# Fetching the experts' slots by indirect DMA from normed rows in DRAM, in place of one-hot products

## The chip, the cores and the metric

The kernel runs on one core of one Trainium2 chip. The metric is the device time of one execution in microseconds (us). Before the change it was 2628.83 us, the median of 3 runs (2625.51 to 2629.55).

## What is computed

Two transformer blocks on 512 tokens of width 1024, all in float32. The first has a mixer of four kinds of heads and then a mixture of 32 experts; the second has two attention layers. The change touches the mixture of experts alone. Cut to what matters:

```python
def moe(h, router_w, router_b, w_up, b_up, w_down, b_down):      # h: 512 tokens x 1024
    logits = xt @ router_w + router_b                            # 32 experts
    top_vals, top_idx = lax.top_k(logits, 4)                     # 4 experts a token
    gates = softmax(top_vals)
    ...                                                          # sort the token-expert pairs by expert
    def expert_block(e, xb):                                     # xb: the rows of the expert's tokens
        hu = xb @ w_up[e] + b_up[e]                              # 1024 x 2048
        g = minimum(hu[:, :1024], 7.0); lin = clip(hu[:, 1024:], -7.0, 7.0)
        return ((lin + 1.0) * g * sigmoid(1.702 * g)) @ w_down[e] + b_down[e]   # 1024 x 1024
    y = segment_sum(y_rows * row_gate, row_tok)
```

The input `h` is an RMS-normed row, scaled and shifted per channel.

## The kernel before

**Stages.** By the profile's clock the first mixer runs to about 395 us, the experts from there to about 1560 us, the second block to the end. Every expert's weights (12 pieces of 128 x 2048 float32, 1 MB each: 8 for the up product, 4 for the down product) are read from HBM once. SyncE's queue issues these loads (`load_piece`, L201 to L208) in a fixed order. A piece goes to the next of 8 buffers in turn: 2 with the tag `w`, 6 with the tag `w2` (`NW2=6`).

**Kinds of experts.** Experts are ranked by their number of tokens. The first 17 ranks have 128 slots ("wide"), the others 64 ("thin"), and rank 1 has 128 and 64 more ("both"). A wide expert's products (`expert_mm`, L1278 to L1280) use the three-product split: each half piece of weights is cut into a high part by ScalarE (L1262) and a low part by VectorE (L1263), in 3 + 1 buffers each. A thin expert (`thin_mm`, L1292) multiplies the float32 pieces straight from their load buffers, which are thus free when TensorE is done with them.

**Order of the work.** `moe_groups` pairs ranks: one wide unit alone, three pairs wide and thin, one pair "both" and thin, four pairs, one wide alone, seven pairs. For each unit, `moe` issues the first half of the up product, then the down product of the unit before it, then the second half of the up product (`expert_up`, `expert_down`). In the last unit of each group, between that down product and the second half, `make` calls `slot_sets` for the next group. So it is called 16 times in this loop, 14 times in a thin unit and twice in a wide one (the first unit and the wide unit that stands alone), and once ahead of it.

**What `slot_sets` does.** The normed rows of all tokens are kept on chip as a high and a low part, in the tiles `aTh` and `aTl` (2 x 16 KB of each partition; written at L988, L989). For each set a one-hot matrix of tokens against slots is made on VectorE (L1177). 64 matmuls (8 channel chunks, 4 token tiles, 2 parts; L1192) then multiply rows by one-hot columns into four PSUM tiles. ScalarE evicts them with scale and shift (L1200); for a wide set ScalarE and VectorE split the outcome again (L1204, L1205). After the second half of the up product, `slot_index` finds each slot's token and gate with small matmuls (L1219, L1223) and VectorE operations (L1228 to L1233).

**The results.** `expert_down` adds each unit's rows to the output in DRAM with an indirect accumulating DMA from GpSimd's queue (L1376).

**Order on each engine.** The framework that builds the program orders instructions per engine ahead of time by what it reckons to be ready, so neighbouring steps of the listing are interleaved: in the trace the high parts of the next wide unit are made in the midst of the evictions of `slot_sets`.

Of the kernel before, what the change touches and what calls it, by code (L numbers as in the profile page):

```python
# [12 lines left out]
F32 = mybir.dt.float32  # L13
# [7 lines left out]
P = 128  # L21
# [65 lines left out]
class Kern:  # L87
# [13 lines left out]
    def run(self):  # L101
        with self.early():
            self.consts()
            with self.phase("first", NW2=1, NHT=17, NHD=8, NP=8):
                x = self.first_mixer()
            with self.phase("moe", NW2=6, NP=1):
                x, aT, late = self.moe(x)
        with self.phase("second", NW2=0, NHD=19, NP=11):
            self.second_block(x, aT, late)
# [5 lines left out]
        return ctx  # L115

    def phase(self, name, **sizes):
        self.wrr = -1
# [746 lines left out]
    def first_mixer(self):  # L865
# [58 lines left out]
        for k in range(KC):  # L924
# [238 lines left out]
    def width(kind):  # L1163
        return C if kind == "wide" else CN

    def slot_sets(self, sets, mid=iter(())):


        nc = self.nc
        next(mid, None)  # L1170
        n = sum(self.width(kind) for kind, *_ in sets)
        oh = self.t([P, NT, 2 * C], F32R, tag="eoh", bufs=1)[:, :, 0:n]
        xs, at, o = [], [], 0
        for kind, R, *_ in sets:
            w = self.width(kind)
            sh = [P, NT, w]
            nc.vector.tensor_tensor(oh[:, :, o:o + w], self.C["iota1"][:, None, 0:w].to_broadcast(sh),  # L1177
                                    R[:, :, None].to_broadcast(sh), op=OP.is_equal)
            if kind == "wide":
                xs.append(self.t([P, 2, KC, C], F32R, tag="xT", bufs=1))  # L1180
            else:
                xs.append(self.t([P, KC, CN], tag="xN", bufs=3))
            at.append(slice(o, o + w))
            o += w
        next(mid, None)
        for k0, bank in zip(range(0, KC, 2), ("tr", "tr", "o", "o2")):
            pt = self.psum(bank)
            for q in range(2):
                k = k0 + q
# [4 lines left out]
            if k0 == 2:  # L1194
                next(mid, None)
            for (kind, *_), x, a in zip(sets, xs, at):
                f = self.t([P, 2, C], tag="ef", bufs=2) if kind == "wide" else x[:, k0:k0 + 2, :]
                for q in range(2):
                    k = k0 + q
                    nc.scalar.activation(f[:, q], pt[:, q * n + a.start:q * n + a.stop], AF.Identity,  # L1200
                                         scale=self.s2[:, k:k + 1], bias=self.b2[:, k:k + 1])
                if kind == "wide":
                    hi, lo = (x[:, m, k0:k0 + 2, :] for m in range(2))
                    nc.scalar.activation(hi, f, AF.Copy)  # L1204
                    nc.vector.tensor_tensor(lo, f, hi, op=OP.subtract)  # L1205

        def index():
            for (kind, _, tok, dst, gate), a in zip(sets, at):
                self.slot_index(kind, oh[:, :, a], tok, dst, gate)
        return xs, index  # L1210

    def slot_index(self, kind, oh, tok, dst, gate):


        nc = self.nc
# [9 lines left out]
        u = self.t([P, 1], tag="six", bufs=2)  # L1225
        if kind == "wide":
            dump = self.C["dump"]
            nc.vector.tensor_scalar(u, v[:, 1:2], dump, None, op0=OP.mult)  # L1228
            nc.vector.scalar_tensor_tensor(dst, v[:, 0:1], dump, u, op0=OP.add, op1=OP.subtract)
        else:  # L1230
            nc.vector.tensor_scalar(u, v[:, 1:2], self.C["ndd"], self.C["dn2"], op0=OP.mult, op1=OP.add)
            nc.vector.scalar_tensor_tensor(dst, v[:, 0:1], 2.0, u, op0=OP.mult, op1=OP.add)
        nc.vector.tensor_reduce(gate, v[:, 2:4], axis=AXX, op=OP.add)  # L1233
# [172 lines left out]
    def moe(self, xin):  # L1406
# [8 lines left out]
        gates = self.t([P, nset], tag="eix2", bufs=1)  # L1415
        cols = {}

        def make(g, R, tok, mid=iter(())):
# [10 lines left out]
            xs, index = self.slot_sets(sets, mid)  # L1429
            xs = iter(xs)  # L1430
            return {pos: [(kind, next(xs)) for kind, _ in kinds] for pos, kinds in g}, index

        def load(pos, ns):
            if pos not in ex:
# [13 lines left out]
        xs, index = make(groups[0], self.R, self.tok, order)  # L1448
        index()
        for _ in bias:  # L1450
            pass
        starts = {g[-1][0]: n + 1 for n, g in enumerate(groups)}
        prev = None
        for n, (pos, kinds) in enumerate(units):
            aT = []

            def mid():
                aT.extend((kind, self.expert_aT(a) if kind == "wide" else self.thin_aT(a)) for kind, _, a in prev[1])
            sets = [(kind, x, self.t([P, D], tag="ea", bufs=1) if kind == "wide" else self.t([P, 512], tag="eat", bufs=1))
                    for kind, x in xs[pos]]  # L1460
            self.expert_up(0, sets, w, pos, mid if prev else None)
            if not n:
                for _ in order:
                    pass
            if prev:
                self.moe_down(prev[0], aT, load(prev[0], range(8, 12)), cols, dsts, gates)
            g = starts.get(pos)
            if g is not None and g < len(groups):
                more, index = make(groups[g], self.Rp, self.tokp)
                xs.update(more)  # L1470
            else:
                index = None
            wu = load(pos, range(4, 8))
            self.expert_up(1, sets, wu, pos)
            if index:
                index()
            if n == 2:
                self.moe_jobs()
            if n + 1 < len(units):
# [20 lines left out]
    def moe_overflow(self):  # L1500
# [5 lines left out]
        with tc.For_i(0, n, 1):  # L1506
# [5 lines left out]
            xs, index = self.slot_sets([("wide", R, tok, dst, gate)])  # L1512
            index()
# [814 lines left out]
```

## Time and profile before

| | |
|---|---|
| median of 3 runs | 2628.83 us (2625.51 to 2629.55) |
| the profiled execution's own time | 2645.91 us |
| its span, first to last instruction | 2644.0 us |
| TensorE matmul busy (x 15499) | 2512.5 us, 95% of the span |
| VectorE busy | 1768.8 us, 67% |
| ScalarE busy | 1258.2 us, 48% |
| GpSimd busy | 154.2 us, 6% |
| mean granted TensorE clock | 0.929 of full speed |
| moved by DMA | 566.51 MB |

The times below come from one profiled execution, which was 17 us longer than the median of the runs. "Busy" of TensorE counts pipelined matmuls with modelled ends, so the starts of neighbouring matmuls tell their real pace. "Idle before" is the time an engine stood still ahead of an instruction, with what ended it. [...] "DMA share" is the mean busy share of the 16 DMA engines.

### The profile page before, as it was taken

To read this page: it belongs to the slowest core of one execution; us is meant where nothing else is said; L and a number is where in the kernel's file an instruction comes from. 1 tells how busy PE (TensorE), PEld (TensorE's weight loads), DVE (VectorE), ACT (ScalarE), POOL (GpSimd) and SP (SyncE) were. 2 spreads that over 40 slices of the span, in tenths; PEclk is the share of its full clock that TensorE was granted. 3 is DMA by queue.
4 is the path that set the end of the run, shared out by engine and by line. 5 is a ranking of instruction groups with operands and counts; after the bars stand their busy time and mean duration, and the time that the engine had idled before them with its cause. 6 is when DMAs were issued, how large, how long until landed. Compare 5 with 4: busy or idle time off the path is not lost.

```text
span 2644.0 us, 40335 instructions
## 1 busy us (share of the span) xinstructions
PE 2512.5 (95%) x15499; PEld 1988.1 (75%) x15499; DVE 1768.8 (67%) x3369; ACT 1258.2 (48%) x2198; POOL 154.2 (6%) x151
## 2 busy tenths in 40 slices
PE   5998879999999999999999969989999999899998
PEld 5875678777677777777777748777777987777778
DVE  6886666766556665866666645687786656877864
ACT  3443546545345554654445534454554444545542
POOL 1001000100000000100000000010000100100001
PEclk9998788999999999999999979999999999999998
DMA  7531237999789999999999962131112431311124
GB/s 294 200 118 68 69 118 291 347 379 370 285 330 377 377 376 376 350 367 378 374 378 372 380 255 84 50 112 67 64 43 86 163 109 51 111 64 64 43 85 144
DMA packets 85828, 566.51 MB, mean 214 GB/s; under 512 B 9984, under 2 KB 10576, under 8 KB 22144
## 3 DMA queue, kind: packets, MB, share of 16 engines
q1 hardware_dynamic: 76368, 536.55, 52.3%
q0 software_dynamic: 7968, 23.90, 3.8%
q10 hardware_dynamic: 1296, 3.44, 0.3%
q8 instruction: 124, 2.03, 0.3%
q14 instruction: 72, 0.59, 0.1%
HBM read 543.93 MB, written 19.92 MB: 213 GB/s over the span
## 4 chain that ended last, share of the span: by engine, by line
PE 71%; DVE 8%; ACT 2%; issue 2%; POOL 1%; DMA 1%; ACTq 0%; POOLq 0%; DVEq 0%
PE mm L1292 5%; PE s L1292 5%; PE mm L395 5%; PE mm L397 5%; PE mm L396 4%; PE o L1292 4%; PE mm L1278 3%; PE o L1278 3%; PE o L1192 2%; PE tr L1192 2%; PE mm L1279 2%; PE mm L1280 2%; PE s L1278 2%; PE o L1280 2%; PE o L1279 2%; PE s L1279 2%
## 5 line engine op out<-in xcount | busy, mean ns | idle before, releaser
L1262 ACT ACTIVATE wh<-w 128x1024 fp32r<-128x1024 f32 x306 | 317.6, 1061 | 292.8 <-PE mm L1279 185.1
L1263 DVE TENSOR_TENSOR wl<-w,wh 128x1024 fp32r<-128x1024 f32 x306 | 367.3, 1220 | 98.8 <-ACT wh L1262 97.2
L214 DVE TENSOR_TENSOR wl<-w,wh 128x1024 fp32r<-128x1024 f32 x194 | 237.1, 1225 | 157.3 <-ACT wh L213 155.4
L213 ACT ACTIVATE wh<-w 128x1024 fp32r<-128x1024 f32 x194 | 205.1, 1060 | 240.0 <-PE mm L372 111.8
L371 PE MATMUL mm<-wl,aTh 128*128 128x256 f32 x816 | 234.7, 288 | 3.5 <-DVE wl L214 3.5
L370 PE MATMUL mm<-wh,aTh 128*128 128x256 f32 x816 | 234.5, 289 | 1.4 <-ACT wh L213 0.6
L372 PE MATMUL mm<-wh,aTl 128*128 128x256 f32 x816 | 235.0, 289 | 0.8 <-DVE aTl L308 0.8
L395 PE MATMUL mm<-aTh,wh 128*128 128x512 f32 x560 | 225.8, 403 | 1.1 <-DVE hd L431 1.1
L397 PE MATMUL mm<-aTh,wl 128*128 128x512 f32 x560 | 223.5, 399 | 0.0
L396 PE MATMUL mm<-aTl,wh 128*128 128x512 f32 x560 | 222.7, 398 | 0.0
L371 PEld LDWEIGHTS mm<-wl,aTh 128*128 128x128 f32 x816 | 157.8, 193 | 6.4 <-DVE wl L214 4.1
L370 PEld LDWEIGHTS mm<-wh,aTh 128*128 128x128 f32 x816 | 157.3, 193 | 5.1 <-issue 1.7
L372 PEld LDWEIGHTS mm<-wh,aTl 128*128 128x128 f32 x816 | 157.3, 193 | 4.3 <-issue 2.7
L459 ACT ACTIVATE P<-s,smx 128x256 f32<-128x256 f32 (+3 forms) x176 | 92.7, 527 | 79.2 <-DVE smx L456 77.5
L1263 DVE TENSOR_TENSOR spl<-w,sph 128x1024 fp32r<-128x1024 f32 x102 | 124.5, 1221 | 0.4 <-ACT sph L1262 0.4
L395 PEld LDWEIGHTS mm<-aTh,wh 128*128 128x128 f32 x560 | 105.9, 189 | 23.0 <-issue 3.8
L1292 PE MATMUL mm<-w,xN 128*64 128x256 f32 x1024 | 122.5, 393 | 0.0
L1321 DVE TENSOR_SCALAR eg<-s 128x512 f32<-128x512 f32 (+1 forms) x66 | 37.0, 561 | 127.5 <-PE s L1282 92.7
L1292 PE MATMUL s<-w,xN 128*64 128x256 f32 x1024 | 122.0, 392 | 0.0
L397 PEld LDWEIGHTS mm<-aTh,wl 128*128 128x128 f32 x560 | 105.7, 189 | 21.6 <-issue 2.0
L1262 ACT ACTIVATE sph<-w 128x1024 fp32r<-128x1024 f32 x102 | 108.2, 1061 | 26.3 <-PE mm L1279 11.6
L396 PEld LDWEIGHTS mm<-aTl,wh 128*128 128x128 f32 x560 | 105.9, 189 | 18.9 <-issue 1.1
(614 smaller groups left out, 5981.5 us busy)
## 6 DMA issues: line engine op xcount, KB each, us to landing
w<-w_exp SPq DMA_DIRECT2D x384, 1024.0 KB, 9.2
w<-w_in SPq DMA_DIRECT2D x57, 1024.0 KB, 4.9
w<-w_out SPq DMA_DIRECT2D x24, 1024.0 KB, 4.9
w<-ada_w SPq DMA_DIRECT2D x19, 1024.0 KB, 4.9
w<-cmp_w SPq DMA_DIRECT2D x8, 1024.0 KB, 4.8
w<-w_up SPq DMA_DIRECT2D x16, 512.0 KB, 3.3
xm<-hd POOLq DMA_DIRECT2D x5, 512.0 KB, 2.9
aTl<-ada_w SPq DMA_DIRECT2D x2, 1024.0 KB, 8.0
```

The costliest lines, as they stand in the source:

```text
L213: self.nc.scalar.activation(hi, src, AF.Copy)
L214: (self.nc.gpsimd if pool else self.nc.vector).tensor_tensor(lo, src, hi, op=OP.subtract)
L370: nc.tensor.matmul(v[:, q, :], ah[k][:, ts], w_h, start=(k == 0), stop=False)
L371: nc.tensor.matmul(v[:, q, :], ah[k][:, ts], w_l, start=False, stop=False)
L372: nc.tensor.matmul(v[:, q, :], al[k][:, ts], w_h, start=False, stop=(k == kk - 1))
L395: nc.tensor.matmul(ps, w_h, ah[k], start=(k == 0), stop=False)
L396: nc.tensor.matmul(ps, w_h, al[k], start=False, stop=False)
L397: nc.tensor.matmul(ps, w_l, ah[k], start=False, stop=(k == kk - 1))
L1262: nc.scalar.activation(hi, w, AF.Copy)
L1263: (nc.gpsimd if n in self.LO_POOL else nc.vector).tensor_tensor(lo, w, hi, op=OP.subtract)
L1278: nc.tensor.matmul(ps, xh[:, k, :], wh[:, q, :], start=(k == 0), stop=False)
L1292: nc.tensor.matmul(ps[CN * c:CN * (c + 1), 0:256], a, w[:, c * 256:(c + 1) * 256], start=(n == 0), stop=(n == len(jobs) - 1))
```

## The change

- When the rows are normed, GpSimd also writes each normed row tile in float32 to a new DRAM tensor `xg` (512 x 1024).
- The first set is made as before, with one-hot products (`first_set`). After it the two tiles `aTh` and `aTl` hold no rows any more, and are used as four more weight buffers (`self.more`). `NW2` goes from 6 to 4, so there are 10 buffers instead of 8.
- For every other group, `slot_rows` finds the slots' tokens (one-hot matrix, `slot_index`) and fetches their rows by an indirect DMA from `xg`: 128 rows of 4 KB for a wide set; for a thin one 128 half rows of 2 KB, the two halves of 64 tokens. This is done one group ahead, after the second half of the last unit's up product.
- `slot_sets` then only transposes the fetched rows on TensorE (8 transposes for a wide set, 4 for a thin one, into PSUM tiles `tr`, of which there are 2) and evicts them as before. It is called inside the second half of the up product, between its two PSUM banks.

```diff
-            with self.phase("moe", NW2=6, NP=1):
+            with self.phase("moe", NW2=4, NP=1):
...
     def load_piece(self, src):
         self.wrr += 1
-        if self.wrr % (self.NW + self.NW2) < self.NW:
+        n = self.wrr % (self.NW + self.NW2 + len(self.more))
+        if n < self.NW:
             w = self.g([P, 2048], F32, "w", self.NW)
+        elif n < self.NW + self.NW2:
+            w = self.t([P, 2048], tag="w2", bufs=self.NW2)
         else:
-            w = self.t([P, 2048], tag="w2", bufs=self.NW2)
+            w = self.more[n - self.NW - self.NW2]
...
+        self.xg = self.dp.tile([S, D], F32, name=self.nm("xg"), tag="xg")
...
             for q, x in enumerate(xs):
-                hi, lo = (r[:, 2 * tp + q, :] for r in self.rows)
+                t = 2 * tp + q
+                xr = self.row()
+                nc.gpsimd.tensor_scalar(xr, x, rs[:, q:q + 1], None, op0=OP.mult)
+                nc.gpsimd.dma_start(self.xg[t * P:(t + 1) * P, :], xr)
+                hi, lo = (r[:, t, :] for r in self.rows)
...
+    def first_set(self, R, tok, dst, gate, mid):
...
+        for k0, bank in zip(range(0, KC, 4), ("tr", "o")):
+            pt = self.psum(bank)
+            for q in range(4):
                 for t in range(NT):
                     for m, r in enumerate(self.rows):
-                        nc.tensor.matmul(pt[:, q * n:(q + 1) * n], r[:, t, k * P:(k + 1) * P], oh[:, t],
+                        nc.tensor.matmul(pt[:, q * C:(q + 1) * C], r[:, t, (k0 + q) * P:(k0 + q + 1) * P], oh[:, t],
...
+            self.wide_parts(pt, k0, out)
+        self.slot_index("wide", oh, tok, dst, gate)
...
+    def wide_parts(self, pt, k0, out):
+        f = self.t([P, 4, C], tag="eg2", bufs=1)
+        for q in range(4):
+            k = k0 + q
+            nc.scalar.activation(f[:, q], pt[:, q * C:(q + 1) * C], AF.Identity, scale=self.s2[:, k:k + 1],
+                                 bias=self.b2[:, k:k + 1])
+        hi, lo = (out[:, m, k0:k0 + 4, :] for m in range(2))
+        nc.scalar.activation(hi, f, AF.Copy)
+        nc.vector.tensor_tensor(lo, f, hi, op=OP.subtract)
+
+    def slot_rows(self, sets):
+        out = []
+        for kind, R, tok, dst, gate in sets:
+            n = self.t([P, 1], I32, tag="eig", bufs=4)
+            self.slot_index(kind, self.one_hot(kind, R), tok, dst, gate, n)
+            if kind == "wide":
+                x, rows = self.t([P, D], tag="xgw", bufs=1), self.xg
+            else:
+                x, rows = self.t([P, 512], tag="xgn", bufs=2), self.xg.rearrange("r (c d) -> (r c) d", c=2)
+            self.nc.gpsimd.indirect_dma_start(out=x, out_offset=None, in_=rows,
+                                              in_offset=bass.IndirectOffsetOnAxis(ap=n, axis=0))
+            out.append((kind, x))
+        return out
+
+    def slot_sets(self, got):
+        out = []
+        for kind, x in got:
+            if kind == "wide":
+                out.append(self.wide_x())
+                for k0 in range(0, KC, 4):
+                    pt = self.psum("tr")
+                    for q in range(4):
+                        nc.tensor.transpose(pt[:, q * P:(q + 1) * P], x[:, (k0 + q) * P:(k0 + q + 1) * P], self.ident)
+                    self.wide_parts(pt, k0, out[-1])
+            else:
+                out.append(self.t([P, KC, CN], tag="xN", bufs=3))
+                pt = self.psum("tr")
+                for q in range(4):
+                    nc.tensor.transpose(pt[:, q * P:(q + 1) * P], x[:, q * P:(q + 1) * P], self.ident)
+                for k in range(KC):
+                    o = k % 4 * P + k // 4 * CN
+                    nc.scalar.activation(out[-1][:, k], pt[:, o:o + CN], AF.Identity, scale=self.s2[:, k:k + 1],
+                                         bias=self.b2[:, k:k + 1])
+        return out
...
     def slot_index(self, kind, oh, tok, dst, gate, src=None):
...
+            if src is not None:
+                nc.vector.tensor_copy(src, v[:, 0:1])
...
+        places = [self.g([P, 2, 2048], F32, tag, 1) for tag in ("aTh", "aTl")]
+        self.more = [v[:, n] for v in places for n in range(2)]
...
+            def slots():
+                xs.update(make(groups[g], got))
...
             self.expert_up(0, sets, w, pos, mid if prev else None)
             if not n:
                 for _ in order:
                     pass
+                got = self.slot_rows(sets_of(groups[1], self.Rp, self.tokp))
             if prev:
                 self.moe_down(prev[0], aT, load(prev[0], range(8, 12)), cols, dsts, gates)
-            g = starts.get(pos)
-            if g is not None and g < len(groups):
-                more, index = make(groups[g], self.Rp, self.tokp)
-                xs.update(more)
-            else:
-                index = None
+            g = starts.get(pos, len(groups))
             wu = load(pos, range(4, 8))
-            self.expert_up(1, sets, wu, pos)
-            if index:
-                index()
+            self.expert_up(1, sets, wu, pos, slots if g < len(groups) else None)
+            if g + 1 < len(groups):
+                got = self.slot_rows(sets_of(groups[g + 1], self.Rp, self.tokp))
```

## Rows read from the trace of the kernel before

**Rows 1.** The page: the 40 slices, busy tenths of TensorE, DMA tenths, GB/s.
```profile
PE   5998879999999999999999969989999999899998
...
DMA  7531237999789999999999962131112431311124
GB/s 294 200 118 68 69 118 291 347 379 370 285 330 377 377 376 376 350 367 378 374 378 372 380 255 84 50 112 67 64 43 86 163 109 51 111 64 64 43 85 144
```
**Rows 2.** Busy time by stretch: one steady pair of units, then cut in three.
```profile
core 0: us, PE busy (x) PEld busy (x) DVE busy (x) ACT busy (x) POOL busy (x), PEclk, DMA share, GB/s
876.60:945.45 68.85, 68.85 (x453) 52.12 (x452) 43.02 (x58) 34.55 (x52) 3.10 (x2) 0.95 0.97 379
...
876.60:883.90 7.30, 7.30 (x67) 7.19 (x65) 2.43 (x4) 5.21 (x13) 1.55 (x1) 0.95 1.02 380
883.90:893.20 9.30, 9.30 (x93) 6.22 (x92) 6.20 (x11) 5.58 (x14) 0.00 (x0) 0.95 0.79 267
893.20:945.40 52.20, 52.20 (x300) 38.70 (x297) 34.40 (x45) 23.75 (x27) 1.55 (x1) 0.95 1.00 399
```
**Rows 3.** Waits, 500 to 1560 us (total us, times, longest): SyncE's queue; ScalarE.
```profile
SPq L208 <- PE mm L1292: 267.2, 60, 11.6
SPq L208 <- DVE wl L1263: 177.8, 48, 10.6
...
ACT wh L1262 <- DMA w<-w_exp: 35.4, 25, 6.0
```
**Rows 4.** Timeline of TensorE: the slot products of that pair, first and last of 64.
```profile
876.61 0.25 PE L1192 MATMUL tr<-eoh,aTh 128*128 128x192 f32 x1
...
883.67 0.27 PE L1192 MATMUL o<-eoh,aTl 128*128 128x192 f32 x1
883.87 3.81 PE L1292 MATMUL mm<-w,xN 128*64 128x256 f32 x32
```
**Rows 5.** Timeline of TensorE: eight and four transposes of float32 tiles, and what follows.
```profile
860.05 1.11 PE L1348 MATMUL tr<-cstident,ea 128*128 128x128 f32 x8
861.09 3.81 PE L1292 MATMUL s<-w,xN 128*64 128x256 f32 x32
...
830.31 0.61 PE L1331 MATMUL tr<-cstident,eat 128*128 128x128 f32 x4
...
830.67 0.48 PE L1278 MATMUL s<-wh,xT 128*128 128x512 f32 x1
```
**Rows 6.** Timeline of ScalarE: evictions of a slot set, and weights between them.
```profile
880.39 0.81 ACT L1200 ACTIVATE ef<-tr,mod,s 128x128 f32<-128x128 f32 x2
...
881.97 2.96 ACT L1262 ACTIVATE wh<-w 128x1024 fp32r<-128x1024 f32 x3
```
**Rows 7.** Stretches: the pair with "both"; the lone wide unit; the one after it.
```profile
642.90:738.80 95.90, 95.90 (x682) 68.55 (x681) 49.67 (x73) 42.46 (x68) 5.38 (x3) 0.95 0.76 279
...
1014.20:1049.80 35.60, 35.60 (x259) 26.91 (x258) 21.84 (x31) 18.14 (x28) 1.55 (x1) 0.95 0.95 348
1049.80:1127.20 77.40, 76.80 (x420) 61.17 (x419) 58.80 (x73) 49.51 (x66) 9.52 (x2) 0.95 0.94 355
...
1060.00:1100.00 40.00, 39.40 (x188) 31.49 (x187) 39.07 (x50) 32.25 (x42) 3.47 (x1) 0.95 0.87 334
```
**Rows 8.** GpSimd's indirect DMAs: time on its queue, and from issue to landing.
```profile
L1376 POOL DMA_INDIRECT xm<-eyn,eix x1: 1550/1550/1550, 913.7 to 913.7; - x1
...
DMA to landing us min/median/max: 8.6/9.5/10.5
```
**Rows 9.** Timeline, 379 to 398 us: the end of the first mixer and the first slots.
```profile
379.58 2.19 ACT L988 ACTIVATE aTh<-hd,rsy 128x1024 fp32r<-128x1024 f32 x2 [2.03 <-DVE rsy L240]
385.88 0.86 POOL L1075 COPY rG<-rtok 128x64 f32<-128x64 f32 x3 [14.14 <-DVE rtok L1071]
...
390.02 0.53 POOL L995 DMA_DIRECT2D xm<-hd  x1 [3.27 <-DVE hd L1088]
...
394.62 0.69 DVE L1177 TENSOR_TENSOR eoh<-cstlt,rR 128x512 fp32r<-128x512 f32 x1 [3.27 <-DMA xm<-hd]
...
395.71 2.16 POOL L1445 COPY g2n<-g2b 64x512 f32<-64x512 f32 x2
```
**Rows 10.** Stretches by rate and clock: a run of loads alone; the start of the experts.
```profile
924.00:948.00 24.00, 24.00 (x155) 17.92 (x154) 14.87 (x18) 9.99 (x13) 1.31 (x1) 0.95 1.01 422
...
372.00:396.00 24.00, 9.86 (x40) 7.16 (x38) 15.18 (x49) 7.63 (x13) 2.75 (x8) 0.57 0.23 91
396.00:416.00 20.00, 17.73 (x81) 17.12 (x82) 7.15 (x25) 5.84 (x13) 3.20 (x6) 0.50 1.00 398
```
**Rows 11.** The chain of waits that ended last: 32 slot products at either clock.
```profile
405.92 7.02 PE o L1192 x32
434.40 3.58 PE tr L1192 x32
```

More of the change, by code (lines that the diff above doesn't have):

```diff
@@ L117, in phase @@
     def phase(self, name, **sizes):
-        self.wrr = -1
+        self.wrr, self.more = -1, []
         for k, v in sizes.items():
@@ L1164, in width, with one_hot, wide_x @@
         return C if kind == "wide" else CN
-    def slot_sets(self, sets, mid=iter(())):
+    def one_hot(self, kind, R):
+        w = self.width(kind)
+        oh = self.t([P, NT, C], F32R, tag="eoh", bufs=2)[:, :, 0:w]
+        sh = [P, NT, w]
+        self.nc.vector.tensor_tensor(oh, self.C["iota1"][:, None, 0:w].to_broadcast(sh), R[:, :, None].to_broadcast(sh),
+                                     op=OP.is_equal)
+        return oh
+    def wide_x(self):
+        return self.t([P, 2, KC, C], F32R, tag="xT", bufs=2)
@@ L1169, in slot_sets @@
+    def first_set(self, R, tok, dst, gate, mid):
         nc = self.nc
         next(mid, None)
[L1171 to L1180, printed above, removed]
-            else:
-                xs.append(self.t([P, KC, CN], tag="xN", bufs=3))
-            at.append(slice(o, o + w))
-            o += w
+        oh = self.one_hot("wide", R)
+        out = self.wide_x()
@@ L1185, in slot_sets @@
         next(mid, None)
-        for k0, bank in zip(range(0, KC, 2), ("tr", "tr", "o", "o2")):
+        for k0, bank in zip(range(0, KC, 4), ("tr", "o")):
             pt = self.psum(bank)
-            for q in range(2):
-                k = k0 + q
+            for q in range(4):
                 for t in range(NT):
                     for m, r in enumerate(self.rows):
-                        nc.tensor.matmul(pt[:, q * n:(q + 1) * n], r[:, t, k * P:(k + 1) * P], oh[:, t],
+                        nc.tensor.matmul(pt[:, q * C:(q + 1) * C], r[:, t, (k0 + q) * P:(k0 + q + 1) * P], oh[:, t],
@@ L1193, in slot_sets @@
                                          start=(t == m == 0), stop=(t == NT - 1 and m == 1))
-            if k0 == 2:
+            if not k0:
                 next(mid, None)
[L1196 to L1212, printed above, removed]
+            self.wide_parts(pt, k0, out)
+        self.slot_index("wide", oh, tok, dst, gate)
+        return out
+    def wide_parts(self, pt, k0, out):
+        nc = self.nc
+        f = self.t([P, 4, C], tag="eg2", bufs=1)
[6 more added lines that the diff above has]
+        nc.vector.tensor_tensor(lo, f, hi, op=OP.subtract)
@@ new lines, in slot_sets @@
+    def slot_sets(self, got):
+        nc = self.nc
+        out = []
[16 more added lines that the diff above has]
+                                         bias=self.b2[:, k:k + 1])
+        return out
@@ L1215, in slot_index @@
+    def slot_index(self, kind, oh, tok, dst, gate, src=None):
         nc = self.nc
@@ L1230, in slot_index @@
         else:
+            if src is not None:
+                nc.vector.tensor_scalar(src, v[:, 0:1], 2.0, self.second, op0=OP.mult, op1=OP.add)
             nc.vector.tensor_scalar(u, v[:, 1:2], self.C["ndd"], self.C["dn2"], op0=OP.mult, op1=OP.add)
@@ L1416, in moe, with sets_of @@
         cols = {}
-        def make(g, R, tok, mid=iter(())):
+        def sets_of(g, R, tok):
             sets = []
@@ L1428, in make @@
                     sets.append((kind, r, tok[:, :, pos, :], dsts[:, n:n + 1], gates[:, n:n + 1]))
-            xs, index = self.slot_sets(sets, mid)
-            xs = iter(xs)
-            return {pos: [(kind, next(xs)) for kind, _ in kinds] for pos, kinds in g}, index
+            return sets
+        def make(g, got):
+            out = iter(self.slot_sets(got))
+            return {pos: [(kind, next(out)) for kind, _ in kinds] for pos, kinds in g}
         def load(pos, ns):
@@ L1447, in moe @@
         order = self.order_ranks()
-        xs, index = make(groups[0], self.R, self.tok, order)
-        index()
+        self.second = self.t([P, 1], tag="second", bufs=1)
+        nc.vector.tensor_tensor(self.second, self.C["ndd"], self.C["dn2"], op=OP.add)
+        (_, *first), = sets_of(groups[0], self.R, self.tok)
+        xs = {0: [("wide", self.first_set(*first, order))]}
         for _ in bias:
             pass
+        places = [self.g([P, 2, 2048], F32, tag, 1) for tag in ("aTh", "aTl")]
+        self.more = [v[:, n] for v in places for n in range(2)]
         starts = {g[-1][0]: n + 1 for n, g in enumerate(groups)}
@@ L1464, in moe @@
                     pass
+                got = self.slot_rows(sets_of(groups[1], self.Rp, self.tokp))
             if prev:
                 self.moe_down(prev[0], aT, load(prev[0], range(8, 12)), cols, dsts, gates)
-            g = starts.get(pos)
-            if g is not None and g < len(groups):
-                more, index = make(groups[g], self.Rp, self.tokp)
-                xs.update(more)
-            else:
-                index = None
+            g = starts.get(pos, len(groups))
             wu = load(pos, range(4, 8))
-            self.expert_up(1, sets, wu, pos)
-            if index:
-                index()
+            self.expert_up(1, sets, wu, pos, slots if g < len(groups) else None)
+            if g + 1 < len(groups):
+                got = self.slot_rows(sets_of(groups[g + 1], self.Rp, self.tokp))
             if n == 2:
@@ L1511, in moe_overflow @@
             e = nc.sync.value_load(ei[0:1, 0:1], min_val=0, max_val=NE - 1)
-            xs, index = self.slot_sets([("wide", R, tok, dst, gate)])
-            index()
+            xs = self.slot_sets(self.slot_rows([("wide", R, tok, dst, gate)]))
             sets = [("wide", xs[0], self.t([P, D], tag="ea", bufs=1))]
```

## The prediction

> **What bounds the kernel now.** I read the page's slices first. In slices 8 to 23 TensorE stands at 9 tenths throughout, and the DMA engines at 7 to 9, at 285 to 380 GB/s [rows 1]. That is the stage of the experts, and two resources look full, so the question is which of them ends last. Next I cut one steady pair of units into stretches. TensorE has no idle time in its 68.85 us, at the upper clock; the DMA share is 0.97, but it drops to 0.79 and 267 GB/s in the 9.3 us of the thin unit's second half [rows 2]. The waits say why: SyncE's queue stands waiting for a buffer that TensorE's thin products or VectorE's split still read (267.2 us behind one line alone), while ScalarE waits for a load only 25 times, 35.4 us in all [rows 3], and TensorE stands still nowhere in the pair. So TensorE is the bound, and the loads are a close second that waits for it.
>
> **What goes.** The slot products of a pair start at 876.61 us, and the next product after them starts at 883.87 us [rows 4]. By starts, the honest measure, that is 7.26 us on TensorE, with nothing beside them there. There are 16 such blocks in the loop; the one ahead of it stays.
>
> **What comes on TensorE.** Eight transposes take 861.09 - 860.05 = 1.04 us from start to start, four take 830.67 - 830.31 = 0.36 us [rows 5]: 1.4 us a pair. The net is 7.26 - 1.4 = 5.86 us. The small index matmuls stay.
>
> **A new wait.** The three PSUM tiles of a pair's transposes share two buffers, so the third can start only when ScalarE has evicted four columns of the first, 2 x 0.81 = 1.6 us [rows 6], while the second is transposed in about 0.5 us. [...] I take 0.5 us, nearer to nothing, since TensorE shows no idle time in the pair today. ScalarE and VectorE evict as much as before; with 34.55 and 43.02 us of work in 68.85 [rows 2] they have room in a pair, and the 2.96 us of weight splits in the midst of the evictions [rows 6] show that the order bends round them. The net is 5.4 us a pair, 63.5 us left; 14 pairs give 75 us.
>
> **The two calls in wide units.** Between 1060 and 1100 us, where two wide units follow each other, VectorE is busy 39.07 of 40 us [rows 7]. A shorter TensorE does not shorten that. I take 1.5 us there, between 0 and 5.9. The first group's rows can't be fetched a group ahead: index, 1.55 us on GpSimd's queue, then 9.5 us to landing [rows 8] stand against the 7 us of products that go, so I count 0 there, between -7 and 5.
>
> **The start.** GpSimd gets four scalings of 128x1024. It has no such row; a copy of 64x512 took 2.16 / 2 = 1.08 us [rows 9], so twice the length makes about 2.1 us. Two of them with their DMA issues (0.53 us each) make 5.3 us from 379.58 us, done at 384.9, just ahead of the gate copies that GpSimd starts at 385.88, and behind those wait the rows that the first slot set waits for until 394.62 us [rows 9]. If nothing covers them they cost 5.3 us. Six buffers are loaded early instead of eight, and the other four come free when the first set's products end near 413 us; the loads run at 398 GB/s there [rows 10]. I take 2 us for the start, between 0 and 8. The last use of the four buffers lies ahead of the tail, which keeps its time.
>
> **What the transfers allow.** A pair loads 24 pieces of 1.049 MB, 25.17 MB, and adds 0.79 MB of results; the fetch brings another 0.79 MB (512 KB and 256 KB), so 26.75 MB. At the 422 GB/s of a stretch of loads alone [rows 10] that is 63.4 us, at the 399 GB/s of a stretch with a result DMA in it [rows 2] 67.0 us. I take 66.0, nearer to the second because every pair has such DMAs and now a fetch. That is 2.5 us more than TensorE needs, so the transfers would come to bound a pair in the long run. But ten buffers hold 25 us of loads; four serve the products in hand and some two the splits ahead of them, which leaves about 10 us of lead. It is full ahead of the loop. Three pairs use 7.5 us of it; in the pair with "both" the DMA share is 0.76 over 95.9 us, so it fills again; four pairs use 10 us; the lone wide unit and the one after it take 35.6 + 77.4 us, enough to fill most of it [rows 7]; the last six use 15 us. By that 5 to 7 us are lost, with no lead 13 x 2.5 = 32 us. I take 14 us.
>
> [...]
>
> **The sum.** 75 + 1.5 + 0 - 2 - 14 = 60 us less. Against the profiled execution's 2645.9 us that is 2586 us. That execution was 17 us above the median of the runs, 2628.8 us, and against the median I forecast 2569 us.
>
> **The rivals.**
> 1. The transfers bound every pair, with no lead to speak of. For it: a DMA share of 0.97 already; a fetch of scattered rows; the four new buffers are halves of two tiles, and if a load into one half waits for readers of the other, the extra depth is lost. Against it: 422 GB/s when the queue is full. At 67.0 us a pair 14 x 1.85 = 26 us are won, less 2 at the start: 2605 us. Rates between 399 and 405 GB/s give 2592 to 2605. [...]
> 2. Slower: TensorE stands at the transposes, for the fetched rows or for the evictions, long enough for its clock to fall. At the start it did little for 24 us and was then granted 0.50 through the first set [rows 10]: 32 products took 7.02 us where they take 3.58 at the upper clock [rows 11]. Per pair a stand of 2 us and 12 us at half clock (6 us lost) make 8 against 5.9 won: 16 x 2.1 = 34 us slower, 2663 us. It decides once stand and lost clock pass 5.9 us a pair. Against it: a fetch has some 60 us to land, six times the 9.5 us of [rows 8], and the 0.6 us of idle time in the 77.40 us stretch of [rows 7] did not move the clock.
> 3. No change: the time freed on TensorE is given back in the same stretch, because the second half of the thin unit now waits for its loads. The drop to 267 GB/s there speaks for it, as it is where the queue catches its breath; that its cause is a missing buffer, of which there are now two more, speaks against it. 2629 us.
>
> **How the numbers follow.** The forecast, with 40 to 84 us won, has a chance of 0.60; the full 16 x 5.9 us less hardly anything, over 84 us, 0.02. Rival 1, from 6 to 40 us won, has 0.27, rival 3 0.04 and rival 2 0.07. So faster is 0.89, the same 0.04, slower 0.07; 0.2% or 5 us is about what a measurement of this kernel can tell from none. The range runs from 2545 us, where nothing is lost to the transfers and little to waits, to 2612 us, which takes in rival 1 down to 17 us won. It leaves out rivals 2 and 3 and the ends.
>
> **What the changed profile would show.** Right: the slot products only ahead of the loop; pairs of 63 to 66 us; twelve transposes a pair, some 1.4 us from start to start; a DMA share of 0.97 or more in the stretch of the thin unit's second half; 16 more fetches of each kind on GpSimd's queue; the clock at 0.95 through the experts. TensorE's first idle gaps should end on a load, and stand in the later pairs of each run. Wrong: pairs at 67 us with gaps at loads in all of them (rival 1); gaps at the transposes and a clock of 0.50 (rival 2); gaps in the second block, or a start of the experts later than 400 us, for which I have no term.

## The result, and the profile after

The changed kernel takes 2660.4 us (median of 4 runs, 2655.6 to 2662.9) against 2629.1 us for the one before: a ratio of 1.012, 95% interval 1.0102 to 1.0137. It is slower by 31 us where 60 us less were forecast, and outside the range.

One number of the trace before has to be put right first. Its profiled execution lay 17 us above the median, with an upper clock recorded as 0.95 (column PEclk, the granted TensorE clock as a share of full speed). Every later profile records 1.00, and in one of a kernel that takes the same time as the kernel before (experiment 8) the steady pair takes 67.90 us where [rows 2] have 68.85. So 67.9 us is the pair to compare with.

The page of the changed kernel, the lines that answer to [rows 1]:

```profile
PE   5998878999999998999999969989999999899998
...
DMA  7531238999899999999999962122112531221124
GB/s 287 203 124 62 79 140 326 368 361 384 316 346 399 375 386 355 374 383 376 370 371 373 379 253 84 65 80 94 52 48 80 174 111 50 98 77 59 45 88 143
```

By these lines nothing seems wrong: TensorE at 9 tenths, the DMA engines full. The stretches of two steady pairs say more (columns as in [rows 2]):

```profile
1220.85:1292.45 71.60, 67.00 (x401) 47.40 (x401) 42.77 (x59) 34.18 (x50) 8.34 (x4) 0.95 0.97 374
1292.45:1364.05 71.60, 66.99 (x401) 47.42 (x401) 42.77 (x59) 34.19 (x50) 8.34 (x4) 0.95 0.97 374
```

The pair has 52 matmuls fewer (401 for the 453 of [rows 2]) and takes 71.6 us. TensorE now stands 4.6 us of it, where it stood none, and the mean clock is 0.95 of an upper 1.00. VectorE and ScalarE are as busy as before. The five costliest of the waits of TensorE from 460 to 1540 us (total us, times, longest), of which the kernel before had one line of 0.9 us in all, name what it stands for:

```profile
PE mm L1331 <- DVE wl L1314: 15.6, 24, 1.1
PE tr L1382 <- DVE eat L1374: 13.7, 14, 1.1
PE tr L1270 <- DVE eix L1284: 12.8, 8, 1.6
PE tr L1251 <- ACT eg L1213: 5.0, 12, 0.4
PE tr L1245 <- DMA xgw<-xg,eig: 3.9, 1, 3.9
```

L1331 is the product with the low weights, L1382 the transposes of the thin set's activations, L1270 the index products. All three end on VectorE. The wait that I had in mind, for the bank of the third transposes (L1251), is the fourth, 0.4 us at a time; the fetched rows are late once, and once more, by 4.7 us, for the first group, ahead of this stretch. No load of weights is among them.

The timeline of ScalarE (start, us, what; the idle time before it in brackets) shows what VectorE itself was waiting for:

```profile
1259.26 0.60 ACT L1402 ACTIVATE eah<-tr 128x512 fp32r<-128x512 f32 x1 [9.41 <-PE tr L1399]
...
1261.01 1.50 ACT L1213 ACTIVATE eg<-tr,mod,s 128x128 f32<-128x128 f32 x4 [0.85 <-DVE eg L1373]
1262.54 0.63 ACT L1216 ACTIVATE xT<-eg 128x512 fp32r<-128x512 f32 x1
...
1264.14 1.51 ACT L1213 ACTIVATE eg<-tr,mod,s 128x128 f32<-128x128 f32 x4
...
1266.61 2.04 ACT L1313 ACTIVATE wh<-aTh 128x1024 fp32r<-128x1024 f32 x2
```

ScalarE first stands 9.41 us, waiting in its queue for a transpose. Then it evicts the new transposes from 1261.01 to 1266.61 without a pause, and only then comes to the first weights of the down product. In the kernel before, three weight splits stood in the midst of the evictions [rows 6]; here 13 of the 16 evictions come first, and two splits stand ahead of the last three. The transposes use only the "tr" banks, so nothing ties them to the down product as the bank "o" tied half of the slot products; that this is why they were put ahead of it is my reading, which no run shows. On TensorE in the same stretch:

```profile
1265.70 0.61 PE L1266 MATMUL tr<-orT,eoh 128*128 128x4 f32 x4 [0.17 <-ACT eg L1213]
1267.90 1.02 PE L1270 MATMUL tr<-orT,eoh 128*64 128x4 f32 x16 [1.60 <-DVE eix L1284]
1268.86 0.80 PE L1329 MATMUL o<-wh,eah 128*128 128x512 f32 x1
```

The thin set's index waits for a bank that VectorE reads (L1284) at the end of 1.3 us of work in its queue, which began only when ScalarE's eviction had let the wide set's index products (L1266) go. And then the clock (stretches, as in [rows 2]):

```profile
1250.00:1258.00 8.00, 8.00 (x51) 5.44 (x51) 3.44 (x5) 0.00 (x0) 0.00 (x0) 1.00 1.02 420
1262.00:1267.60 5.60, 3.69 (x30) 2.29 (x28) 2.38 (x7) 5.48 (x15) 0.83 (x1) 1.00 1.01 404
1267.60:1274.40 6.80, 6.50 (x29) 5.32 (x30) 6.80 (x13) 5.30 (x9) 3.60 (x2) 0.50 0.91 334
```

TensorE is without pause in the first of these stretches and stands for 1.9 us of the second, in three pieces; then the granted clock goes from 1.00 to 0.50 for 6.8 us. No pause ahead of the fall is longer than 1.6 us. The trace has eleven such falls in the experts, 51 us together; the kernel before has none between 417 and 1558 us. In this pair 13 products of 512 columns start 0.43 us apart instead of 0.234, and 16 index products take 0.95 us instead of 0.57: some 3 us lost (an estimate from these rows). So a pair gives back its 7.26 us, and 3.7 more: 4.6 us of standing, some 3 us at half clock, 1.5 us of transposes, and some 2 us that no single row names.

### The profile page after: what moved, and what is told of

Its sections match the earlier page's. It is cut to its first block, busy times and chain, and to the rows that moved or that the text cites. A ratio compares the mean times of both kernels' runs of the same rounds, so it can differ in the third digit from the quotient of the medians.

```text
span 2659.8 us, 38716 instructions
## 1 busy us (share of the span) xinstructions
PE 2453.9 (92%) x14667; PEld 1891.5 (71%) x14667; DVE 1768.7 (66%) x3368; ACT 1249.0 (47%) x2164; POOL 223.8 (8%) x191
## 5 line engine op out<-in xcount | busy, mean ns | idle before, releaser
L217 DVE TENSOR_TENSOR wl<-w,wh 128x1024 fp32r<-128x1024 f32 x194 | 237.2, 1225 | 153.3 <-ACT wh L216 151.6
L216 ACT ACTIVATE wh<-w 128x1024 fp32r<-128x1024 f32 x194 | 205.0, 1059 | 237.6 <-PE mm L375 110.6
L1314 DVE TENSOR_TENSOR wl<-w,wh 128x1024 fp32r<-128x1024 f32 x186 | 220.8, 1217 | 19.8 <-ACT wh L1313 18.2
L1313 ACT ACTIVATE wh<-w 128x1024 fp32r<-128x1024 f32 x186 | 191.6, 1064 | 59.4 <-PE mm L1330 25.9
L1402 ACT ACTIVATE eah<-tr 128x512 fp32r<-128x512 f32 x34 | 20.1, 596 | 238.3 <-PE tr L1399 236.3
L1371 ACT ACTIVATE eg<-eg 128x512 f32<-128x512 f32 (+1 forms) x66 | 34.8, 527 | 159.1 <-DVE eg L1370 155.4
L1331 PE MATMUL mm<-wl,xT 128*128 128x512 f32 x204 | 84.7, 415 | 15.9 <-DVE wl L1314 15.6
L1370 DVE TENSOR_SCALAR eg<-mm 128x512 f32<-128x512 f32 (+1 forms) x66 | 37.0, 561 | 93.0 <-PE mm L1343 90.1
```

What stands on the lines that cost most here:

```text
L216: self.nc.scalar.activation(hi, src, AF.Copy)
L217: (self.nc.gpsimd if pool else self.nc.vector).tensor_tensor(lo, src, hi, op=OP.subtract)
L1313: nc.scalar.activation(hi, w, AF.Copy)
L1314: (nc.gpsimd if n in self.LO_POOL else nc.vector).tensor_tensor(lo, w, hi, op=OP.subtract)
L1331: nc.tensor.matmul(ps, xh[:, k, :], wl[:, q, :], start=False, stop=(k == KC - 1 and not bias))
```

## The experiments

The theory, from these rows: **the turn**. I took ScalarE and VectorE each to work off their queue in order; of VectorE experiment 1 shows it, with 2.30 us of idle time while the inputs of the split behind were there. At three places of a pair TensorE goes from a thin unit's products to a wide unit's, which need split weights; there the queues hold, ahead of the splits, evictions that wait for TensorE's last thin products. When I set up the experiments I took the slot products to be the time in which these engines came round. Rivals: **the transfers** (the pair waits for its loads, the fetch crowding them) and **the buffers** (the new places are given back late). Line numbers shift a little between the kernels.

**1. The kernel before with an eighth of the slot products.** No other step of the program is edited; 56 of 64 products are left out.

```
                     for m, r in enumerate(self.rows):
+                        if t or m:
+                            continue
...
```

> The kernel before, with 8 of the 64 slot products of a set (the 8 of the first tile and half) and the other 56 left out; nothing else is changed, so its slots hold partial rows and the output differs. It asks what the TensorE time that the change frees is worth when no order and no transfer changes. If the loads would bound the freed pair (theory of the transfers), a pair cannot fall under the 26.75 MB at 399 to 422 GB/s, 63.4 to 67.0 us, in place of 68.85: 2 to 5 us of each of 14 pairs, 2555 to 2600 us. If TensorE's order is what cost the change its gain (theory of the order), nothing stands in the way here: 56 products at 7.26 us by 64 are 6.35 us a set, 15 sets, 95 us less: 2535 us, with TensorE still without a gap and its clock up through the experts.

Measured: 2608.0 us, 0.992 (0.991 to 0.994), much less than either theory gave. Some 12 of the 22 us lie ahead of the experts' first product, which starts at 401.9 us in place of 413.6, as the first set loses products too. A steady pair, its stretch and pieces of ScalarE's and VectorE's timelines:

```profile
1246.00:1313.70 67.70, 64.22 (x399) 45.38 (x398) 43.28 (x59) 34.40 (x52) 3.84 (x2) 1.00 1.00 384
```

```profile
1263.15 2.94 ACT L1264 ACTIVATE wh<-w 128x1024 fp32r<-128x1024 f32 x3
...
1266.27 0.48 DVE L1375 SCALAR_TENSOR_TENSOR eyn<-o,eix,g2n 128x256 f32<-128x256 f32 x1 [2.30 <-PE o L1294]
1266.67 2.35 DVE L1265 TENSOR_TENSOR wl<-w,wh 128x1024 fp32r<-128x1024 f32 x2
```

6.35 us of products are gone and the pair is 0.2 us shorter than 67.9. With no fetch and no new transposes, at full clock, TensorE stands 67.70 - 64.22 = 3.5 us. The other 2.7 us no single row names, and how they were lost was not shown. How TensorE comes to stand VectorE shows: it idles 2.30 us for the thin down product's end, although the high halves of the next weights have been there since 1264.2 us, evicts, and then begins the split that TensorE needs at once. It is the turn, without the rest of the change; that it would cost nearly all that was freed I had not expected.

But more than the products has changed here: the framework has put the queues in another order. The same entry in the kernel before, on VectorE:

```profile
1296.35 2.35 DVE L1263 TENSOR_TENSOR wl<-w,wh 128x1024 fp32r<-128x1024 f32 x2
1298.62 0.47 DVE L1373 SCALAR_TENSOR_TENSOR eyn<-o,eix,g2n 128x256 f32<-128x256 f32 x1
1299.02 1.21 DVE L1263 TENSOR_TENSOR spl<-w,sph 128x1024 fp32r<-128x1024 f32 x1
1301.35 0.48 DVE L1373 SCALAR_TENSOR_TENSOR eyn<-o,eix,g2n 128x256 f32<-128x256 f32 x1 [1.13 <-PE o L1292]
```

There the splits stand ahead of the thin unit's last eviction, and they run under thin products: the slot products of that pair start only at 1333.85 us, behind the wide down product, and stand at none of the three entries. Counted over the experts, the first low split of a wide section is queued ahead of the thin unit's last eviction at all 46 entries of the kernel before, at 7 of 47 in this run, and at 8 of 47 in the changed kernel. So the turn came with the new order, and the slot products did not cover it. Why the framework orders the queues otherwise when the products are gone stays open.

**2. The changed kernel, transposes no earlier than written.** `self.last` is the last product recorded.

```
+                with self.tc.issue_after(self.last.ins):
                     xs.update(make(groups[g], got))
...
+                with self.tc.issue_after(self.last.ins):
                     got = self.slot_rows(sets_of(groups[g + 1], self.Rp, self.tokp))
```

> The changed kernel, with two edges of order on TensorE alone: the slots' transposes may not pass the last product that was written ahead of them (the thin unit's second half), and the index transposes not the end of that half. Theory of the order: the evictions of the transposes no longer stand ahead of the splits of the down products' weights, the waits on the index (1.7 us a pair), on the low weights and on the thin set's transpose shrink, but the transposes still interleave with the thin unit's tanh: a pair at 66 to 69 us in place of 71.5, 2580 to 2630 us. Theory of the transfers (the fetch's 12 indirect rows sets and the loads share the queues, and the pair waits for its loads): the order of TensorE does not matter, 2650 to 2670 us. Theory of the buffers (the ten raw-weight buffers are given back late): no change either, 2650 to 2670 us.

Measured: 2662.7 us, 1.013 (1.011 to 1.015). A miss for my theory as it then was, and inside the range of both rivals, which experiment 4 takes up: I had thought only of what the transposes pass. The index waits shrank, and those for low weights grew from 18.4 to 35.3 us.

**3 and 4. The transposes behind the down product; the same without the fetch.**

```
-            self.expert_up(1, sets, wu, pos, slots if g < len(groups) else None)
+            if g < len(groups):
+                slots()
+            self.expert_up(1, sets, wu, pos)
```

> As the run before it, but the slots' transposes are written directly behind the thin unit's down product of its first half, ahead of the second half, so that they stand at one place, with 12 transposes of some 2.2 us, and their evictions lie under the second half's products. Theory of the order: TensorE has no long wait left, its clock stays up, and a pair takes 68.85 - 7.26 + 2.2 = 63.8 us at TensorE, or what the loads allow (63.4 to 67.0): 2560 to 2600 us. Theories of the transfers and of the buffers: 2650 to 2670 us, as the changed kernel.

> As the run before it, without the indirect fetches of the pairs' rows: the transposes read two tiles that are loaded once, so the slots hold other rows and the output differs; index work, transposes, evictions and order stay. Theory of the order: within 0.5% of the run before it, since the fetch has 9.5 us to land in and nobody waits for it. Theory of the transfers: the fetch costs its pair 2 us or more, so this one is 30 us or more faster than the run before it.

Measured: 2640.2 us, 1.0046 (1.003 to 1.006), and without the fetch 2633.7 us, 1.0016 (1.0006 to 1.0026). A steady pair of each:

```profile
1201.10:1269.80 68.70, 64.30 (x403) 45.41 (x401) 42.77 (x59) 34.35 (x50) 12.99 (x5) 1.00 1.01 388
```

```profile
1200.90:1269.70 68.80, 64.40 (x404) 45.53 (x402) 42.85 (x59) 34.36 (x50) 3.84 (x2) 1.00 0.99 380
```

Without the fetch the whole is 6.5 us shorter, but not the steady pair: the transfers are not what holds it. The place of the transposes is worth 20 us, not 60 to 100. What is left, in the waits of the first of the two:

```profile
PE mm L1331 <- DVE wl L1314: 24.8, 23, 1.6
PE o L1331 <- DVE wl L1314: 17.8, 13, 1.6
```

36 waits for the low weights, 42.6 us of the 54 us of all its waits, at the entries into wide sections: the turn of experiment 1.

**5 to 8. The turn taken away.** The first two splits of a wide section are written, and on VectorE queued, ahead of the thin unit's last eviction; the loads that they need are issued earlier. In experiment 5 the index and the thin set's transposes also go behind the next wide section's first bank.

```
+    def split_ahead(self, pieces):
+        self.ahead = [self.moe_split(*h) for h in self.half_pieces(pieces[:1])]
+        return self.tc.issue_after(self.low.ins)
...
+            with self.split_ahead(then) if then else ExitStack():
                 nc.vector.tensor_scalar(l, pl[:, 0:w], SWIGLU_LIMIT, -SWIGLU_LIMIT, op0=OP.min, op1=OP.max)
                 nc.vector.scalar_tensor_tensor(a[:, half * w:(half + 1) * w], l, 1.0, g, op0=OP.add, op1=OP.mult)
...
             def mid():
+                with self.tc.issue_after(self.last.ins):
+                    middle()
+                    if later:
+                        got[:] = self.slot_rows(sets_of(later.pop(), self.Rp, self.tokp))
```

> The kernel with the transposes behind the down product, and two further edits of order: the first two weight splits of a wide section are written, and on VectorE queued, ahead of the thin unit's last eviction there (which waits for TensorE's last thin product); the index work and the thin set's transposes are put behind the first bank of the next wide section. Theory of the turn (VectorE stands in its queue for the thin product's end, so the low weights come 1.1 to 1.5 us after TensorE is free, three times a pair, and the freed time goes into that): 2.7 us of waits in front of the up products and 1.9 us in front of the down products go, a pair falls from 68.7 to 64 to 65 us, 2565 to 2590 us. Theory of the transfers (the loads bound the pair whatever the order; the even 67.6 us of the pairs with fewer products, and 68.7 here, are the loads' pace): no change within 0.3%, 2630 to 2645 us.

> The changed kernel with the splits ahead alone; its transposes, their evictions and the index stay where they were. Theory of the turn: the waits for the low weights (1.6 us a pair) go, the index's and the thin set's waits (2.7 us) and most of the falls of the clock (3 us) stay: 2630 to 2650 us. Theory of the transfers: 2655 to 2665 us.

> The kernel before with 8 of 64 slot products (56 left out, so the output differs) and the splits ahead. Theory of the turn: of the 6.35 us a set that were freed and of which 5.2 us went into waits, 2.5 to 4.5 us come out now: a pair of 63 to 65 us in place of 67.6, 2540 to 2570 us. Theory of the transfers: 67.6 us is the pace of 26.75 MB at 396 GB/s, the run stays within 0.3% of the 2608 us of the one without splits ahead.

> The kernel before with the splits ahead and nothing else. Theory of the turn: TensorE has no gap in these pairs, since the 64 products cover VectorE's turn, so the splits gain nothing here: within 0.3% of the kernel before, 2622 to 2638 us. If the splits were worth something by themselves, whatever the products, it would be 20 us or more faster.

Measured, in this order: 2581.2 us, 0.982 (0.980 to 0.9835); 2636.2 us, 1.0025 (1.0015 to 1.0035); 2575.4 us, 0.979 (0.978 to 0.981); 2627.8 us, 0.9995 (0.9986 to 1.0005). A steady pair of experiment 5 and its two last full ones, a steady pair of experiment 7, and one of experiment 8:

```profile
1160.80:1224.00 63.20, 63.08 (x401) 45.69 (x400) 42.82 (x59) 34.15 (x51) 5.87 (x4) 1.00 1.02 408
...
1288.10:1353.40 65.30, 63.72 (x402) 45.44 (x401) 42.75 (x59) 33.91 (x50) 5.89 (x4) 1.00 1.02 409
1353.40:1418.80 65.40, 63.87 (x402) 45.50 (x401) 41.92 (x57) 33.92 (x50) 5.89 (x4) 1.00 1.02 408
```

```profile
1225.20:1290.30 65.10, 63.88 (x397) 45.35 (x396) 43.28 (x59) 34.16 (x53) 3.83 (x2) 1.00 1.01 400
```

```profile
1273.00:1340.90 67.90, 67.90 (x455) 51.81 (x453) 43.05 (x60) 34.56 (x52) 3.10 (x2) 1.00 0.98 383
```

The same edit is worth 33 us where the products are gone (experiment 7 against 1), 24 us in the changed kernel, and nothing in the kernel before. There it finds nothing to do: the splits stood ahead at every entry already. So the zero of experiment 8 agrees with the turn, but it is no sign that products covered it, as I had expected. A loads' bound would have left experiments 5 and 7 where they were; nor can the earlier issue of the loads be the gain, since ScalarE waits for a load only 0.3 us in the whole of the changed kernel's experts. Experiment 7 misses its range by 5 us: 2.8 of the 6.35 us come out, TensorE still waits for low weights at the down product (13 times, 13.5 us in all), and the DMA share is 1.01. Experiment 5 beats both kernels, by 47 and 79 us. VectorE at an entry, now the other way round:

```profile
1179.66 1.22 DVE L1314 TENSOR_TENSOR wl<-aTl,wh 128x1024 fp32r<-128x1024 f32 x1
1181.58 0.48 DVE L1433 SCALAR_TENSOR_TENSOR eyn<-o,eix,g2n 128x256 f32<-128x256 f32 x1 [0.70 <-PE o L1350]
```

In its last pairs the DMA engines are full (share 1.02) and the pair takes 65.4 us: 26.75 MB at 409 GB/s. ScalarE waits for loads, 62.7 us in all:

```profile
ACT wh L1313 <- DMA w<-w_exp: 62.7, 34, 10.3
```

**9 to 12. What is left, and which edit made it.** All start from experiment 5: without the fetch; with one of the two places as buffers; with index and thin transposes where they were; with the slots' transposes where the change has them.

```
-        self.more = [v[:, n] for v in places for n in range(2)]
+        self.more = [v[:, n] for v in places[:1] for n in range(2)]
```

> The kernel with the transposes behind the down product, the splits ahead and the index behind the next bank (2581 us), without the indirect fetches: the transposes read two tiles loaded once, so the output differs. In that kernel the loads become the pace: its last three pairs take 64.0, 65.3 and 65.4 us with the DMA engines full at 408 GB/s, after 63.2 in the pairs before. If the loads' lead is what runs out there, taking 0.8 MB a pair off the engines (2 us of 65.4) keeps all pairs at 63.2: 4 to 8 us less, 2573 to 2577 us. If the late pairs come from the order, the same time within 2 us.

> The same kernel (2581 us) with only one of the two places of the rows as weight buffers, 8 as before the change in place of 10. If the loads are the pace by the end, two buffers less are 2.1 MB less of lead, at 408 GB/s 5 us, lost once, and late pairs begin two pairs earlier: 2584 to 2592 us. If loads don't bind, no change within 0.2%.

> The same kernel (2581 us) with the index work and the thin set's transposes back in front of the wide section; the splits stay ahead. Theory of the turn: the waits on the index and on the thin set's last eviction, now behind two splits on VectorE, come back at 1 to 2 us a pair: 2595 to 2615 us. If the splits alone made the gain: 2580 to 2585 us.

> The same kernel (2581 us) with the slots' transposes written where the change has them, so that they may pass the down product, and their 12 evictions stand on ScalarE ahead of the down product's splits. Theory of the turn: the down product waits for its splits, 1.5 to 3 us a pair, with a fall of the clock: 2605 to 2640 us. If the place of the transposes doesn't matter once the splits go ahead: 2580 to 2585 us.

Measured: 2563.1 us, 0.975 (0.973 to 0.977); 2581.4 us, 0.982 (0.981 to 0.984); 2608.0 us, 0.992 (0.990 to 0.994); 2621.1 us, 0.997 (0.996 to 0.998).

Without the fetch the last full pair is back at 63.2 us:

```profile
1343.50:1406.70 63.20, 63.08 (x401) 45.69 (x401) 41.91 (x57) 34.19 (x51) 3.83 (x2) 1.00 1.02 408
```

So late pairs were the loads', as expected; but 18 us came out where I had put 4 to 8. By the two profiles 15.7 us of it lie in the experts: 5.6 us between the start of the first wide unit and that of the second pair, and 10 us after, mostly in the last four pairs. The 5.6 us do not belong to late pairs: in experiment 5 TensorE stands 4.6 us there, once, for the first rows fetched, and 10.2 us at half clock follow; without the fetch neither is there. The two buffers less cost nothing that can be told by the medians (a miss): ScalarE waits longer for loads, 121.1 us in all, but its last full pair takes 65.8 us, hardly more than 65.4. With four runs each, which scatter over 5 and 6 us, the lower end of the 3 to 11 us expected is not ruled out: by the two profiles it is 1080.2 us in place of 1076.4 from the experts' first product to their last section.

The last two put the order's parts back, one at a time. The index in its place costs 27 us, the transposes in theirs 40 us; in a pair of the latter it is the down product that waits (waits, 460 to 1540 us):

```profile
PE o L1336 <- ACT wh L1313: 23.2, 13, 2.4
PE o L1338 <- DVE wl L1314: 8.3, 17, 0.5
```

ScalarE evicts ahead of the splits, so TensorE waits 23.2 / 13 = 1.8 us a pair, and the clock falls in most pairs, ten times in all. Step by step, the changed kernel's 2660 us become 2640 with the transposes behind the down product, 2608 with the splits ahead, 2581 with the index behind the next bank.

## Why the prediction was wrong, step by step

- **What bounds the kernel**: right for the kernel before. TensorE first, the transfers close behind, as experiment 5 shows once nothing else is in the way.
- **What goes**, 7.26 us: right.
- **What comes**, 1.4 us of transposes: 1.55 us by starts in experiment 5 (0.96 and 0.59), 2.2 in the changed kernel, with the wait for the bank.
- **A new wait**, 0.5 us: this step failed. No row showed the 0.5 us; the wait it names, the third transposes', came at 0.44 us. What failed is the sentence behind it, that ScalarE and VectorE "have room in a pair" and "the order bends round them". Busy time of 34 and 43 us in a pair says nothing of a queue worked off in order: in experiment 1 VectorE idles 2.3 us just ahead of the split that is wanted. And the order did not bend. I took the order of [rows 6], and the lack of idle time on TensorE, for something that the change would leave; they belonged to the one program. With the slot products gone the framework queued the splits behind the thin unit's last eviction at 39 of 47 entries, where it had them ahead at all 46, and moved the index and the thin set's transposes too. The new order, which the forecast put at no cost, made the 4.6 us of standing and the 3 us at half clock: set right by hand in experiment 5, it leaves a pair of 63.20 us with 63.08 us of products, at a clock of 1.00. In experiment 1 it took all but 0.2 of the 6.35 us freed.
- **The two calls in wide units**, 1.5 us: between the first wide unit of that stretch and the next pair, experiment 5 takes 108.9 us and experiment 8 112.6, so nearer 4. For the first group, put at 0, TensorE did wait for the fetch, 4.7 us in the changed kernel, but the stretch from the first wide unit to the second pair takes 108.3 us in both kernels.
- **The start**, 2 us, up to 8: the first product of the experts comes at 415.9 us in place of 413.6. That is in the range, but experiment 8, with the old start, has 415.5, so no cost can be told.
- **What the transfers allow**: 66.0 us a pair were forecast, 65.4 measured with the DMA engines full. The loss of 14 us is of the size of the 18 that the fetch costs in experiment 9, but 5.6 of these lie at the first group, and some 10 in late pairs. What two of the ten buffers add to the lead was too small for experiment 10 to tell.
- **Rival 2**, at a chance of 0.07, is what happened: 2663 us were worked out, 2660 measured. That they lie so near is luck, since its terms were others. Its mechanism was half right: a stand and a lost clock, but 5 and 3 us, not 2 and 6, and for index, low weights and the thin set's activations on VectorE; for the fetched rows only at the two calls in wide units. What I held against it, a stand of 0.6 us that left the clock alone, was a single one; the pair has several of 0.4 to 1.6 us close together.
- **Rival 1** is seen only in the last pairs of experiment 5; rival 3, waits for loads in the thin unit's second half, not in the changed kernel. The forecast of 2569 us was a forecast for a kernel whose order had been made for it: with that, 2581 us.

VectorE's 2.30 us of idle time in experiment 1, with the split's inputs there, are those of a queue worked off in order. Weighed in the forecast, such an order would have raised the question which instruction stands ahead of each split.

How much of the 31 us is the clock's alone was not separated by a run. Experiment 3 gives a price. Its steady pair of 68.70 us is followed by one with 3.4 us at half clock:

```profile
1269.80:1340.00 70.20, 65.80 (x402) 46.54 (x400) 42.85 (x59) 34.34 (x50) 11.86 (x5) 0.98 1.00 382
```

At 1.5 us for 3.4, the 51 us at half clock of the changed kernel would come to an estimated 23 us.

## What to carry to other kernels

Before costing work off a busy engine, ask in what order the queues of the other engines will stand once it is gone. Where a framework makes that order, taking work away can change it: an engine that idles in its queue, and then begins just what the busy engine needs next, is the sign to look for. A control with that work cut short, and nothing else edited, shows what such a loss costs, but compare the order of its queues with that of the kernel before; here it had moved too. Pin by hand the order of work that has lost what held it in place, and put the part that the bound engine needs first ahead of evictions that wait for that engine.

## What the runs showed that was not expected

The clock fell after short stands: in the steady pairs of the changed kernel none ahead of a fall is above 1.6 us, yet the clock fell eleven times in the experts. Experiment 3 has waits of up to 1.6 us too, further apart, three in most pairs, and only four falls, of 30.6 us together.

The upper clock was recorded as 0.95 in the one profile of the kernel before and as 1.00 elsewhere. The products of 512 columns start 0.234 us apart in both; the thin ones, of 256 columns, took 393 ns on the mean in the first and 382 in the other, which is most of the 1 us a pair between them.
